# Block 0 of a hybrid encoder layer: x taken channel-major and unnormalised, and the memory's product moved behind the convolution

## The chip, the cores and the metric

The kernel runs on one core of one Trainium2 chip. The metric is the device time of one execution in microseconds (us); where several executions are given, their median is what counts. Matmuls run on TensorE (PE in the profile), elementwise work on VectorE (DVE), ScalarE (ACT) and GpSimd (POOL); SyncE (SP) issues most transfers. All numbers are float32.

## The reference

One encoder layer on 2048 tokens of 1024 channels. Three mixers read the same normalised input, are gated and added, and an MLP follows. Cut to what the change touches:

```python
h = rmsnorm(x, g_mix)                    # x / rms(x), times a gain for each channel
z = h @ w_in
qk_m, v_m, o_m, i_pre, f_pre, qkv_na, q_mem, gate_pre = jnp.split(z, split_idx, axis=-1)
qk_m = jax.nn.silu(short_conv(qk_m, conv_w, conv_b))       # 5 taps along the tokens
q_na = rmsnorm(q_na[:, :, 0], g_na_q) * (NA_HEAD_DIM ** -0.5)
k_na = rmsnorm(k_na[:, :, 0], g_na_k)
h_mem = memory_cross_attention(q_mem, rmsnorm(mem, g_mem), w_mem_kv, g_mem_q, g_mem_k)
    # k, v = split(mem_n @ w_mem_kv); softmax(q k^T) v over 256 memory tokens, 4 heads of 64
gates = jax.nn.sigmoid(gate_pre).reshape(bsz, s, N_BRANCH, D_MODEL)
y = gates[:, :, 0] * (h_m @ w_proj_mlstm) + gates[:, :, 1] * (h_na @ w_proj_na) \
    + gates[:, :, 2] * (h_mem @ w_proj_mem)
x = x + y @ w_out
return x + jnp.square(jax.nn.relu(rmsnorm(x, g_ffn) @ w_up)) @ w_down
```

1/rms is one number per token, so it commutes with the product by w_in: (x * g) @ w, scaled by 1/rms of the token afterwards, is the same result.

## The kernel before

**Products in three.** Every large product takes both operands as a high and a low part (`hi`, `lo`, written as fp32r: `hi` is the rounded copy, `lo` what is left) and issues three matmuls, hi*hi, hi*lo and lo*hi (lines 242, 243, 244, `mm3`). A weight comes as units of 512 KB: `fetch` loads one into a raw buffer (`wr`, three of them), ACT writes hi (line 185), DVE writes lo (line 186) into a split buffer (`ws`, five of them). `take(4)` hands four units to a group of products, and loads run ahead in the order of a list (`wplan`). A split buffer comes free when the last product that reads it is done.

**Stages.** The 2048 tokens are four blocks of 512. The first phase goes through the blocks; in each block (`block_a`) PE computes, with the block's normalised, transposed x (`hT`, hi and lo): naqk (queries and keys of the neighbourhood attention; four tiles of 128 tokens, 24 products each), four units of the convolution (channel-major, 24 products each, line 697 moves the result to `cz`, then five taps on DVE, lines 705 to 710, and a tanh on ACT, line 709), navm (values of the neighbourhood attention and the memory's queries; two groups for each tile, `ev` from line 537 and `zm`, `zif` from lines 545 and 546), v, the mLSTM's gates for some blocks, and o. A second phase runs the mLSTM with the branch gates (line 625) of two more blocks, blocks 1 and 0, as filling; a third does projections and the MLP. PE's order is written by hand: between the products of a group, `tick` draws work from a list of jobs and from two streams of attention units (one of neighbourhood attention's q and k, one with two lanes of memory units). The other engines' orders come from a scheduler that goes by the order of the program and its dependences.

**x in block 0 and in the others.** Blocks 1 to 3 get x twice: token-major for the sums of squares (line 462), channel-major (`xT`) for the product. 1/rms is spread over all partitions by a product with ones (line 476), x is scaled on DVE (line 431) and split. Block 0 gets x token-major: squares on ACT (line 350), scaling on DVE (line 352), 32 transposes on PE (line 358, in groups of four), and 32 + 32 small moves to hi and lo (lines 363 and 364).

**The start.** The first product is the memory's: `mem_setup` loads memT, splits it into the buffer of `hT` (lines 1174, 1175) and multiplies it with w_mem_kv (48 products into two PSUM banks, named mx) while x of block 0 comes in. Then come naqk's tiles in the order 2, 3, 0, 1. Of the PSUM banks in this phase `mm` has 2, `tr` 3 and `mx` 3. A memory unit (`mem_unit`) takes two mx banks for its scores (12 small products, line 1275), DVE takes the maxima (line 1278), ACT the exponentials (line 1282).

## Time and profile before

| | |
|---|---|
| median of three runs | 2867.02 us (2867.16, 2867.02, 2863.83) |
| profiled execution, its own time | 2865.11 us |
| span of that execution | 2863.4 us |
| PE busy | 2844.4 us, 99% |
| DVE busy | 2046.7 us, 71% |
| ACT busy | 1163.9 us, 41% |
| granted clock, mean | 0.999 |

Times in the profile are microseconds from the start of the span. A row of the timeline gives the start, the duration, the engine, the line of the kernel, what is written and read, and in brackets how long the engine stood idle before it and what released it. A PE row's duration is longer than the time to the next row, since products overlap: what a product costs is the distance of starts, 0.23 us for 512 columns and 0.12 us for 256. A row of the waits gives the total, the number and the longest of the waits of that kind.

### The profile page before, as it was taken

To read this page: it belongs to the slowest core of one execution; us is meant where nothing else is said; L and a number is where in the kernel's file an instruction comes from. 1 tells how busy PE (TensorE), PEld (TensorE's weight loads), DVE (VectorE), ACT (ScalarE), POOL (GpSimd) and SP (SyncE) were. 2 spreads that over 40 slices of the span, in tenths; PEclk is the share of its full clock that TensorE was granted. 3 is DMA by queue.
4 is the path that set the end of the run, shared out by engine and by line. 5 is a ranking of instruction groups with operands and counts; after the bars stand their busy time and mean duration, and the time that the engine had idled before them with its cause. 6 is when DMAs were issued, how large, how long until landed. Compare 5 with 4: busy or idle time off the path is not lost.

```text
span 2863.4 us, 41480 instructions
## 1 busy us (share of the span) xinstructions
PE 2844.4 (99%) x14950; PEld 2355.7 (82%) x14950; DVE 2046.7 (71%) x3522; ACT 1163.9 (41%) x2205; POOL 199.0 (7%) x254
## 2 busy tenths in 40 slices
PE   9999999999999999999999999999999999999999
PEld 7888888888887888888888888888888888888887
DVE  7686865477765555647699888866786998887666
ACT  6464654355544433532343334333223433343331
POOL 3221210011000122310000000000000000000000
PEclk9999999999999999999999999999999999999999
DMA  8686777886899888977444447756773444476553
GB/s 294 210 281 208 248 238 245 263 245 204 281 312 310 266 271 265 308 262 267 121 152 149 149 162 244 242 196 229 256 219 121 152 149 149 162 249 230 196 188 133
DMA packets 345149, 631.70 MB, mean 221 GB/s; under 512 B 29584, under 2 KB 151376, under 8 KB 344944
## 3 DMA queue, kind: packets, MB, share of 16 engines
q1 hardware_dynamic: 344528, 628.79, 66.9%
q8 instruction: 118, 1.93, 0.3%
q14 instruction: 87, 0.71, 0.1%
q10 hardware_dynamic: 416, 0.27, 0.0%
HBM read 452.32 MB, written 176.62 MB: 220 GB/s over the span
## 4 chain that ended last, share of the span: by engine, by line
PE 92%; DVE 3%; DMA 2%; issue 1%; ACT 1%; POOL 0%; SPq 0%; ACTq 0%; DVEq 0%; POOLq 0%
PE mm L242 28%; PE mm L244 27%; PE mm L243 27%; PE tr L1130 2%; DMA wr<-in_w_units_dram 1%; PE pn L902 1%; PE mx L1144 1%; PE mx L1110 1%; PE pn L905 1%; PE mx L911 1%; PE mx L1305 1%; PE tr L1295 1%; PE mx L1275 1%; DVE ws L186 0%; DVE cy L707 0%
## 5 line engine op out<-in xcount | busy, mean ns | idle before, releaser
L242 PE MATMUL mm<-X,ws 128*128 128x512 f32 x896 | 349.5, 390 | 0.2 <-ACT u L1499 0.2
L243 PE MATMUL mm<-X,ws 128*128 128x512 f32 x896 | 348.6, 389 | 0.0
L244 PE MATMUL mm<-X,ws 128*128 128x512 f32 x896 | 348.6, 389 | 0.0
L186 DVE TENSOR_TENSOR ws<-wr,ws 128x1024 fp32r<-128x1024 f32 (+2 forms) x195 | 237.5, 1225 | 124.3 <-ACT ws L185 122.7
L242 PE MATMUL mm<-hT,ws 128*128 128x512 f32 (+1 forms) x776 | 304.8, 393 | 1.4 <-DMA hT<-s_hT 1.4
L244 PE MATMUL mm<-hT,ws 128*128 128x512 f32 (+1 forms) x776 | 301.7, 389 | 0.0
L243 PE MATMUL mm<-hT,ws 128*128 128x512 f32 (+1 forms) x776 | 301.4, 388 | 0.0
L185 ACT ACTIVATE ws<-wr 128x1024 fp32r<-128x1024 f32 (+2 forms) x195 | 204.6, 1055 | 192.6 <-PE mm L244 135.7
L244 PE MATMUL mm<-X 128*128 128x512 f32 x616 | 239.7, 389 | 0.5 <-DVE X L1563 0.5
L242 PE MATMUL mm<-X 128*128 128x512 f32 x616 | 239.7, 389 | 0.0
L243 PE MATMUL mm<-X 128*128 128x512 f32 x616 | 239.6, 389 | 0.0
L242 PE MATMUL mm<-ws,hT 128*128 128x512 f32 (+2 forms) x640 | 226.4, 354 | 2.7 <-ACT ws L185 1.6
L212 ACT ACTIVATE ws<-wr 128x512 fp32r<-128x512 f32 x224 | 133.9, 627 | 232.8 <-PE mm L244 145.6
L243 PE MATMUL mm<-ws,hT 128*128 128x512 f32 (+2 forms) x640 | 223.3, 349 | 2.1 <-DVE ws L186 2.1
L244 PE MATMUL mm<-ws,hT 128*128 128x512 f32 (+2 forms) x640 | 223.6, 349 | 0.1
L1562 ACT ACTIVATE X<-X 128x1024 fp32r<-128x1024 f32 x109 | 115.7, 1062 | 209.4 <-DMA X<-s_s 92.5
L242 PEld LDWEIGHTS mm<-X,ws 128*128 128x128 f32 x896 | 168.2, 188 | 36.0 <-ACT u L1499 0.6
L243 PEld LDWEIGHTS mm<-X,ws 128*128 128x128 f32 x896 | 168.2, 188 | 35.3 <-issue 0.5
L244 PEld LDWEIGHTS mm<-X,ws 128*128 128x128 f32 x896 | 168.2, 188 | 34.8
L1579 DVE TENSOR_TENSOR acc<-acc,mm 128x512 f32<-128x512 f32 x192 | 126.3, 682 | 70.0 <-PE mm L244 70.0
L1563 DVE TENSOR_TENSOR X<-X 128x1024 fp32r<-128x1024 f32 x109 | 132.4, 1222 | 58.0 <-ACT X L1562 57.4
L242 PEld LDWEIGHTS mm<-hT,ws 128*128 128x128 f32 x776 | 146.1, 188 | 31.0 <-issue 2.8
(280 smaller groups left out, 5946.1 us busy)
## 6 DMA issues: line engine op xcount, KB each, us to landing
wr<-in_w_units_dram SPq DMA_DIRECT2D x289, 512.0 KB
s_s<-u SPq DMA_DIRECT2D x32, 1024.0 KB
s_g<-ev SPq DMA_DIRECT2D x96, 256.0 KB
ev<-s_g SPq DMA_DIRECT2D x96, 256.0 KB
s_a<-u SPq DMA_DIRECT2D x96, 256.0 KB
X<-s_s SPq DMA_DIRECT2D x45, 512.0 KB
nab<-in_rpb_dram SPq DMA_DIRECT2D x96, 220.0 KB
xt<-in_w_units_dram SPq DMA_DIRECT2D x32, 512.0 KB
```

The costliest lines, as they stand in the source:

```text
L185: s = nc.scalar.activation(w[:, 0, ks], raw[:, ks], AF.Copy)
L186: v = nc.vector.tensor_tensor(w[:, 1, ks], raw[:, ks], w[:, 0, ks].bitcast(F32), ALU.subtract)
L212: nc.scalar.activation(hi, src, AF.Copy)
L242: mm(out, lhs[0], rhs[0], start=first, stop=False)
L243: mm(out, lhs[0], rhs[1], start=False, stop=False)
L244: mm(out, lhs[1], rhs[0], start=False, stop=last)
L902: mm(pn[h % 2][:, h // 2], pt[:, h], v1[:, h], start=h < 2, stop=first)
L905: mm(pn[h % 2][:, h // 2], qw[hp, h // 2], C[hp, h // 2], start=False, stop=True)
L1130: nc.tensor.transpose(ptp[0:120, j], sb[:, j * 120:(j + 1) * 120], self.ident)
L1562: nc.scalar.activation(hi, src, AF.Copy)
L1563: nc.vector.tensor_tensor(lo, src, hi.bitcast(F32), ALU.subtract)
L1579: nc.vector.tensor_tensor(c, first[t] if first else c, p, ALU.add)
```

## The change

The change has these parts.

- The memory's product is no longer first. `first_loads` loads x of block 0 channel-major (`xT`, 2 MB), times the gain but without 1/rms, and splits it into `hT` (lines 1141 and 1142 of the changed kernel, 8 + 8 moves for each half of the block). `first_tiles` multiplies naqk's tiles 0 and 1 with it in two mx banks, step by step as the weights arrive, then tiles 2 and 3.
- The four transposed tiles of block 0 are gone: no scaling of rows, no transposes on PE, no 32 + 32 small moves. x is still loaded token-major (2 MB) for the sums of squares.
- `first_rms` computes 1/rms, keeps it per token (`r0`, with 0.5/rms in its second half) and spreads it over the partitions with one product with ones (`rb0`), which is also stored and loaded again in the second phase.
- 1/rms goes into block 0's results: as the scale of the moves of navm, v and o, as a factor on the sums of squares and on the scale in the neighbourhood attention's q and k (one more small POOL operation), as a product on DVE with `rb0` in the convolution's move (line 663, before on ACT), and in the 24 gates of block 0 in the second phase as a product on DVE (line 585), with the tanh on ACT behind it, in place.
- The memory's input is loaded by jobs during the convolution (`mem_load`), its 48 products (`mem_kv`) come between the convolution and navm, and its weights stand behind the convolution's in the list. So the memory units of block 0 start later.

```diff
-        out = list(u["w_mem_kv"])
+        out = []
         for b in range(NB):
-            for n in ("naqk", "qk", "navm", "v"):
+            for n in ("naqk", "qk") + ("w_mem_kv",) * (b == 0) + ("navm", "v"):
                 out += u[n]
...
+            rb=d("s_rb", [128, TB]),
...
-    def prep(self, xt, out, junk):
-    def trans_part(self, xh, dst, t, g):
-    def trans(self, xh, dst, t, later=0):
-    def load_norm(self, src, xt=None):
...
-        self.xorder = [(0, t) for t in ORDER_0] + [(b, t) for b in range(1, NB) for t in range(4)]
+        self.xorder = [(b, t) for b in range(1, NB) for t in range(4)]
         self.xhs = []
         self.hT = self.p_h.tile([128, 2, 8, TB], F32R, name="hT", tag="hT", bufs=1)
         self.streams = [self.unit_stream(self.qkq, [(1, 3)]), self.unit_stream(self.memq, [(3,), (3,)]), self.na_stream()]
-        self.mem_setup()
+        w = self.first_loads()
...
+        self.first_tiles(w)
...
-        w = self.take(4)
-        for i, t in enumerate(ORDER_0 if b == 0 else range(4)):
-            if i == 0 or b == 0 and i < 3:
+        rt = lambda t: self.r0[:, t:t + 1] if b == 0 else 1.0
+        w = self.take(4) if b else ()
+        for t in range(4) if b else ():
+            if t == 0:
                 self.trans_x()
-            if b == 0 and i == MEM_R:
-                self.mem_rms()
             p = self.tok_group(hT, w, t)
             z = self.t("zna", [128, 512], 4)
             self.out = nc.scalar.activation(z, p, AF.Copy).ins,
             self.qkq.append(self.na_qk(b, t, z.rearrange("p (a b) -> p a b", b=32)))
+        if b == 0:
+            mem = self.mem_load()
+            self.jobs += [lambda: next(mem, None)] * 16
...
+        if b == 0:
+            self.mem_kv()
...
-            self.out = nc.scalar.activation(s, p, AF.Copy).ins,
+            self.out = nc.scalar.activation(s, p, AF.Copy, scale=rt(t)).ins,
...
-            v = nc.vector.tensor_copy(z, p[:, 0:256])
-            self.out = v.ins, nc.scalar.activation(zif[:, t], p[:, 256:272], AF.Copy).ins
+            v = nc.vector.tensor_scalar(z, p[:, 0:256], rt(t), None, ALU.mult) if b == 0 else nc.vector.tensor_copy(z, p[:, 0:256])
+            self.out = v.ins, nc.scalar.activation(zif[:, t], p[:, 256:272], AF.Copy, scale=rt(t)).ins
...
-            self.out = nc.scalar.activation(s, p, AF.Copy).ins,
+            self.out = nc.scalar.activation(s, p, AF.Copy, scale=rt(t)).ins,
...
-            self.out = nc.scalar.activation(s, p, AF.Tanh, scale=0.5).ins,
+            self.out = nc.scalar.activation(s, p, AF.Tanh, scale=0.5 if b else self.r0[:, 4 + t:5 + t]).ins,
...
-        self.out = self.nc.scalar.activation(s, p, AF.Tanh, scale=0.5).ins,
+        if b == 0:
+            self.out = self.nc.vector.tensor_tensor(s, p, self.rb, ALU.mult).ins,
+            self.nc.scalar.activation(s, s, AF.Tanh, scale=0.5)
+        else:
+            self.out = self.nc.scalar.activation(s, p, AF.Tanh, scale=0.5).ins,
...
+        self.rb = self.gbc[:, 0:TB]
+        nc.sync.dma_start(self.rb, self.scr["rb"])
...
-        self.out = nc.scalar.activation(z[:, 4:4 + TB], p, AF.Copy).ins,
+        if b == 0:
+            self.out = nc.vector.tensor_tensor(z[:, 4:4 + TB], p, self.rb0, ALU.mult).ins,
+        else:
+            self.out = nc.scalar.activation(z[:, 4:4 + TB], p, AF.Copy).ins,
...
-        nc.scalar.activation(sq, z, AF.Square)
+        r0 = self.r0[:, t:t + 1] if b == 0 else 1.0
+        nc.scalar.activation(sq, z, AF.Square, scale=r0)
         ss = self.small(16, "q")
         nc.vector.tensor_reduce(ss, sq, AX.X, ALU.add)
         r = self.rstd(ss, 32, "q")
+        if b == 0:
+            nc.gpsimd.tensor_scalar(r, r, r0, None, ALU.mult)
...
-    def mem_setup(self):
+    def first_loads(self):
...
+        xs = [p_a.tile([128, 4 * 704], F32, name=f"xs{i}", tag="nak", bufs=2)[:, :2 * D].rearrange("p (t c) -> p t c", t=2) for i in range(2)]
+        src = [a["xT"][2 * i:2 * i + 2].rearrange("t p c -> p t c") for i in range(2)]
+        def split(i, k):
+            hi, lo = (self.hT[:, l, k, i * 256:i * 256 + 256].rearrange("p (t c) -> p t c", t=2) for l in range(2))
+            x, g = xs[i][:, :, k * 128:(k + 1) * 128], self.gmix[:, k:k + 1]
+            nc.scalar.activation(hi, x, AF.Copy, scale=g)
+            nc.vector.scalar_tensor_tensor(lo, x, g, hi.bitcast(F32), ALU.mult, ALU.subtract)
         later, self.later = self.later, 0
         for k in range(0, 8, 2):
             if k == 0:
                 self.fetch(2)
...
+            cs = slice(k * 128, k * 128 + 256)
+            (nc.sync if k else nc.scalar).dma_start(xs[0][:, :, cs], src[0][:, :, cs])
             for i in (k, k + 1):
...
+                split(0, i)
             if k:
                 self.fetch()
...
+        for k in range(0, 8, 4):
+            cs = slice(k * 128, k * 128 + 512)
+            nc.sync.dma_start(xs[1][:, :, cs], src[1][:, :, cs])
+        self.later = later
+        self.xr = []
+        for t in range(4):
+            self.n += 1
+            x = self.x_tile(a["x"][t * 128:t * 128 + 128]) if t < 2 else p_a.tile([128, D], F32, name=f"xr{t}", tag="naq", bufs=2)
+            if t > 1:
+                nc.sync.dma_start(x, a["x"][t * 128:t * 128 + 128])
+            self.xr.append(x)
+        for k in range(8):
+            split(1, k)
         w = self.take(4)
...
+        self.r0 = p_a.tile([128, 8], F32, name="r0")
+        return w
+    def first_rms(self):
+        nc = self.nc
+        ss = self.small(4, "x")
+        for t, x in enumerate(self.xr):
+            nc.scalar.activation(x, x, AF.Square, accum_out=ss[:, t:t + 1])
+            yield
+        r = self.rstd(ss, D, "x")
+        nc.gpsimd.tensor_copy(self.r0[:, 0:4], r)
+        nc.gpsimd.tensor_scalar(self.r0[:, 4:8], r, 0.5, None, ALU.mult)
+        yield
+        self.rb0 = self.gbc[:, 0:TB]
+        dg = self.ev().rearrange("p (t c) -> p t c", t=4)
+        nc.vector.tensor_tensor(dg, self.ident.unsqueeze(1).to_broadcast([128, 4, 128]),
+                                r.unsqueeze(2).to_broadcast([128, 4, 128]), ALU.mult)
+        for _ in range(7):
+            yield
+        p = self.ps("tr")
+        nc.tensor.matmul(p, self.ones, dg.rearrange("p t c -> p (t c)"), start=True, stop=True)
+        nc.scalar.activation(self.rb0, p, AF.Copy)
+        self.store(self.scr["rb"], self.rb0)
+    def first_tiles(self, w):
+        nc, hT = self.nc, self.hT
+        rms = self.first_rms()
+        self.jobs += [None] * RMS_0 + [lambda: next(rms, None)] * 13
+        zs = [self.t("zna", [128, 512], 4) for _ in range(4)]
+        unit = lambda t: self.qkq.append(self.na_qk(0, t, zs[t].rearrange("p (a b) -> p a b", b=32)))
         ps = [self.ps("mx") for _ in range(2)]
...
         for k in range(8):
             wk = w[k // 2]
             for t in range(2):
...
+                self.mm3(ps[t], self.lhs_tok(hT, k, t), (wk[:, 0, k % 2], wk[:, 1, k % 2]), k == 0, k == 7)
             self.tick()
...
+        self.out = tuple(nc.scalar.activation(z, p, AF.Copy).ins for z, p in zip(zs, ps))
+        for t in (2, 3):
+            p = self.tok_group(hT, w, t)
+            self.out = nc.scalar.activation(zs[t], p, AF.Copy).ins,
+            unit(t - 2)
+        unit(2)
+        unit(3)
+    def mem_load(self):
+        nc, a, p_a = self.nc, self.a, self.p_a
+        raw = [p_a.tile([128, D], F32, name=f"memT{i}", tag="naq", bufs=2) for i in range(2)]
+        for i in range(2):
+            nc.sync.dma_start(raw[i].rearrange("p (k t) -> p k t", k=4), a["memT"][i * 512:(i + 1) * 512].rearrange("(k p) t -> p k t", p=128))
+        yield
+        mt = [self.x_tile(a["mem"][t * 128:t * 128 + 128]) for t in range(2)]
+        self.memT = [p_a.tile([128, 4 * 704], F32R, name=f"memh{i}", tag="nak", bufs=2)[:, :2 * D].rearrange("p (k t) -> p k t", k=8)
+                     for i in range(2)]
+        for _ in range(MEM_LOAD):
+            yield
+        for k in range(8):
+            x, g = raw[k // 4][:, k % 4 * 256:k % 4 * 256 + 256], self.gmem[:, k:k + 1]
+            hi, lo = (m[:, k] for m in self.memT)
+            nc.scalar.activation(hi, x, AF.Copy, scale=g)
+            nc.vector.scalar_tensor_tensor(lo, x, g, hi.bitcast(F32), ALU.mult, ALU.subtract)
+            yield
+        ss = self.small(2, "x")
+        for t in range(2):
+            nc.scalar.activation(mt[t], mt[t], AF.Square, accum_out=ss[:, t:t + 1])
+        self.rm = self.rstd(ss, D, "m")
+    def mem_kv(self):
+        nc = self.nc
+        w = self.take(4)
+        ps = [self.ps("mx") for _ in range(2)]
+        for k in range(8):
+            wk = w[k // 2]
+            for t in range(2):
+                ts = slice(t * 128, (t + 1) * 128)
+                self.mm3(ps[t], tuple(m[:, k, ts] for m in self.memT), (wk[:, 0, k % 2], wk[:, 1, k % 2]), k == 0, k == 7)
+            self.tick()
+        out = []
         for t, p in enumerate(ps):
             z = self.t("zm", [128, 256], 4)
...
+            out.append(nc.scalar.activation(z, p[:, 0:256], AF.Copy).ins)
+            out.append(nc.vector.tensor_copy(self.mv[:, t], p[:, 256:512]).ins)
+            self.memq.append(self.mem_keys(t, z, self.rm[:, t:t + 1]))
+        self.out = tuple(out)
```

Three places show how the order moves. The first is **PE in naqk of block 0**, between the first tiles in the rows of before (`mm_574` is a tile's PSUM bank, `ws_296` and `ws_301` are weight buffers, `tr_600` a bank of transposed x).

```order
L244 MATMUL mm_574<-ws_296,hT 128x512
L358 MATMUL tr_600<-ident,xstage 128x128 x4
L242 MATMUL mm_574<-ws_301,hT 128x512
L243 MATMUL mm_574<-ws_301,hT 128x512
L244 MATMUL mm_574<-ws_301,hT 128x512
```

In the changed kernel, from the last products of tile 2 to the first of tile 3:

```order
L242 MATMUL mm_421<-ws_268,hT 128x512
L243 MATMUL mm_421<-ws_268,hT 128x512
L241 MATMUL mm_447<-ws_230,hT 128x512
L242 MATMUL mm_447<-ws_230,hT 128x512
L243 MATMUL mm_447<-ws_230,hT 128x512
```

The groups of four transposes are gone, and the weights of tiles 0 and 1 (`ws_230` to `ws_268`) serve tiles 2 and 3 too. The second place is **ACT at the end of block 0's navm**. Before, with `mm_1142` the second group of tile 2, `zif` its move by ACT, `ws_936` to `ws_946` the high parts of v's weights and `mq_1253` the queries of a memory unit:

```order
L1244 ACTIVATE sq_1169<-zm_1106 128x4x64
L546 ACTIVATE zif_955<-mm_1142 128x16
L537 ACTIVATE ev_1221<-mm_1179 128x256
L986 ACTIVATE stq_1020<-tr_1205,gna 128x2x64
L185 ACTIVATE ws_936<-wr_935 128x2x512
L185 ACTIVATE ws_941<-wr_940 128x2x512
L185 ACTIVATE ws_946<-wr_945 128x2x512
L986 ACTIVATE stq_1020<-tr_1205,gna 128x2x64
L1257 ACTIVATE mq_1253<-tr_1254,gmqk 128x256
```

In the changed kernel, with `mm_1053` the second group of tile 2, `ev_1126` the move of tile 3's first group and `mk` the memory's keys:

```order
L496 ACTIVATE ev_1126<-mm_1084,r_332 128x256
L1278 ACTIVATE sq_1163<-zm_952 128x4x64
L1278 ACTIVATE sq_1175<-zm_1018 128x4x64
L184 ACTIVATE ws_832<-wr_831 128x2x512
L184 ACTIVATE ws_837<-wr_836 128x2x512
L184 ACTIVATE ws_842<-wr_841 128x2x512
L1291 ACTIVATE mk<-tr_1158,gmqk 128x2x128
L1291 ACTIVATE mk<-tr_1170,gmqk 128x2x128
L505 ACTIVATE zif_851<-mm_1053,r_332 128x16
```

Tile 2's `zif` stood ahead of the three weights and now stands behind them and behind the keys. The third place is **DVE at the first memory units of block 0**. Before, with `mx_1328` and `mx_1329` the two score banks of the first unit and `mq_1360` the queries of the second:

```order
L1278 TENSOR_REDUCE sm_1342<-mx_1328 128x2
L1278 TENSOR_REDUCE sm_1343<-mx_1329 128x2
L1258 SCALAR_TENSOR_TENSOR mq_1360<-tr_1361,gmqk,mq_1360 128x256
L1286 RECIPROCAL sm_1354<-sm_1344 128x2
L1287 TENSOR_TENSOR me_1348<-me_1348,sm_1354 128x512
```

In the changed kernel, with `mx_1336`, `mx_1337` the banks of the first unit and `mx_1368`, `mx_1369` those of the second:

```order
L1292 SCALAR_TENSOR_TENSOR mq_1284<-tr_1285,gmqk,mq_1284 128x256
L1292 SCALAR_TENSOR_TENSOR mq_1290<-tr_1291,gmqk,mq_1290 128x256
L1312 TENSOR_REDUCE sm_1350<-mx_1336 128x2
L1312 TENSOR_REDUCE sm_1351<-mx_1337 128x2
L1320 RECIPROCAL sm_1362<-sm_1352 128x2
L1321 TENSOR_TENSOR me_1356<-me_1356,sm_1362 128x512
L1320 RECIPROCAL sm_1365<-sm_1353 128x2
L1321 TENSOR_TENSOR me_1359<-me_1359,sm_1365 128x512
L1312 TENSOR_REDUCE sm_1382<-mx_1368 128x2
L1312 TENSOR_REDUCE sm_1383<-mx_1369 128x2
```

The two lanes of memory units, which stood a step apart, now go in step: both queries are there before the first scores, and on PE the 24 score products of two units stand one behind the other, twice in block 0.

More of the change, by code (lines that the diff above doesn't have):

```diff
@@ L431, in prep_x @@
                 nc.vector.scalar_tensor_tensor(xt[:, k], xt[:, k], self.gmix[:, k:k + 1], rb, ALU.mult, ALU.mult)
-            self.xhs.append((xt, t, True))
+            self.xhs.append((xt, t))
     def trans_x(self, later=1):
         if self.xhs:
-            xh, t, major = self.xhs.pop(0)
-            if not major:
-                self.trans(xh, self.hT, t, later)
-                return
+            xh, t = self.xhs.pop(0)
             self.jobs += [None] * (later - len(self.jobs) - 1)
@@ L1196, in mem_setup @@
         nc.vector.tensor_copy(self.gmqk[:, 1:2], gq[:, 1:2])
+        self.gmem = p_a.tile([128, 8], F32, name="gmem")
+        nc.sync.dma_start(self.gmem, a["g_mem"])
         self.mk = p_a.tile([128, 2, 2, 256], F32R, name="mk")
         self.mv = p_a.tile([128, 2, 256], F32, name="mv")
-        ps = [self.ps("mx") for _ in range(2)]
-        self.trans_x(MEM_T)
-        turns = self.jobs[-2:]
-        def turn(f, marks):
-            with self.queued(marks()):
-                f()
-        self.jobs[-2:] = [lambda f=f: turn(f, lambda: first) for f in turns]
-        self.jobs += [lambda i=i: turn(lambda: self.prep_x(xt=xs[:, i * D:(i + 1) * D]), lambda: self.turned + second) for i in range(2)]
+        self.r0 = p_a.tile([128, 8], F32, name="r0")
[26 more added lines that the diff above has]
+        unit = lambda t: self.qkq.append(self.na_qk(0, t, zs[t].rearrange("p (a b) -> p a b", b=32)))
+        ps = [self.ps("mx") for _ in range(2)]
         for k in range(8):
```

72 lines of the change are left out of this document (3 added, 69 removed).

## The prediction

> **What bounds the kernel now.** I read the page's busy times first, then PE's waits, then the windows of the first block, the only stretch in which the order on PE changes much.
>
> ```profile
> span 2863.4 us, 41480 instructions
> PE 2844.4 (99%) x14950; PEld 2355.7 (82%) x14950; DVE 2046.7 (71%) x3522; ACT 1163.9 (41%) x2205; POOL 199.0 (7%) x254
> ```
>
> PE is busy for all but 19 us of the span. An edit gains only what it takes out of PE's products or out of these 19 us. The waits of PE that the change touches (engine, line, releaser: total, times, longest):
>
> ```profile
> PE mm L243 <- DVE ws L186: 2.1, 3, 0.8
> ...
> PE mm L242 <- ACT ws L185: 1.6, 1, 1.6
> PE mx L243 <- DVE ws L186: 1.5, 2, 0.8
> ...
> PE mm L242 <- ACT zif L546: 1.0, 2, 0.8
> ```
>
> The first three say that PE waits for split weights, the fourth that it waits in navm for a PSUM bank to be emptied. Windows of 20 us (window, length, busy PE, PEld, DVE, ACT, POOL, clock, DMA share, GB/s) show where:
>
> ```profile
> 0.00:20.00 20.00, 16.89 (x72) 13.69 (x73) 13.39 (x31) 13.27 (x22) 2.17 (x9) 1.00 0.91 332
> 20.00:40.00 20.00, 17.03 (x76) 13.21 (x75) 13.12 (x33) 15.94 (x36) 7.15 (x9) 0.91 0.77 271
> ...
> 60.00:80.00 20.00, 20.00 (x115) 17.52 (x114) 19.25 (x33) 8.71 (x16) 8.29 (x5) 1.00 0.96 314
> ```
>
> In 0 to 40 us PE is short of weights while the DMA engines are nearly full. From 60 on PE is full, and so nearly is DVE, which does the taps of the convolution there: DVE is the engine that falls behind next.
>
> **Removed: the starvation at the start.** PE's timeline:
>
> ```profile
> 13.10 0.39 PE L242 MATMUL mx<-ws,hT 128*128 128x512 f32 x1
> 14.28 0.50 PE L243 MATMUL mx<-ws,hT 128*128 128x512 f32 x1 [0.79 <-DVE ws L186]
> ...
> 21.70 0.39 PE L244 MATMUL mm<-ws,hT 128*128 128x512 f32 x1
> 23.68 0.49 PE L242 MATMUL mm<-ws,hT 128*128 128x512 f32 x1 [1.59 <-ACT ws L185]
> 24.94 0.80 PE L243 MATMUL mm<-ws,hT 128*128 128x512 f32 x1 [0.77 <-DVE ws L186]
> 25.53 0.63 PE L244 MATMUL mm<-ws,hT 128*128 128x512 f32 x1
> ...
> 27.24 0.87 PE L358 MATMUL tr<-ident,xt 128*128 128x128 f32 x4
> ...
> 29.68 0.48 PE L242 MATMUL mm<-ws,hT 128*128 128x512 f32 x1
> 30.77 0.50 PE L243 MATMUL mm<-ws,hT 128*128 128x512 f32 x1 [0.61 <-DVE ws L186]
> ```
>
> A product costs 0.23. From 13.10 to 14.28 one ran: 0.95 lost. From 21.70 to 27.24 seven ran: 5.54 - 1.61 = 3.93 lost, 1.2 of it since products were 0.43 apart after the two stalls. At 29.68, a product that takes 0.31 behind transposes, 0.78. Together 5.7. Here two groups of weights, eight units, are used up in 26 us. In the changed kernel four units feed all four tiles of naqk, 96 products or 22 us, and the fifth is wanted at about 6 + 22 + 2 = 30. Until then 2 MB of xT, 2 MB of x and five units, 2.5 MB, must come: 6.5 MB at the 332 GB/s of the first window are 20 us. So I take the whole 5.7. The other end: if the loads of x delay the units as much as memT did, half stays, 2.8.
>
> **Removed: 32 transposes, eight groups like this one.**
>
> ```profile
> 16.91 0.60 PE L358 MATMUL tr<-ident,xt 128*128 128x128 f32 x4
> 17.27 0.48 PE L242 MATMUL mx<-ws,hT 128*128 128x512 f32 x1
> 17.58 0.40 PE L243 MATMUL mx<-ws,hT 128*128 128x512 f32 x1
> ```
>
> 0.36 for the group and 0.08 for the slower product behind it make 0.44, times 8: 3.5. Nothing covers PE, so this is certain. The moves and scalings that go with them ran on ACT and DVE beside PE and count nothing by themselves.
>
> **Removed and put back: navm's waits.**
>
> ```profile
> 83.79 0.28 PE L244 MATMUL mm<-ws,hT 128*128 128x256 f32 x1
> 84.25 0.39 PE L242 MATMUL mm<-ws,hT 128*128 128x272 f32 x1 [0.17 <-ACT zif L546]
> ...
> 90.17 0.28 PE L244 MATMUL mm<-ws,hT 128*128 128x256 f32 x1
> 91.29 0.39 PE L242 MATMUL mm<-ws,hT 128*128 128x272 f32 x1 [0.84 <-ACT zif L546]
> ```
>
> Starts of 0.12 would be free, so these cost 0.34 and 1.00, 1.3 in all. With other orders on ACT and DVE the second group of tile 1 now takes the bank that the first group just filled, and its move stands on ACT behind the last unit's tanh, which waits for the taps on DVE. How late are they? Groups of DVE, the first from the page, the others from its first 110 us:
>
> ```profile
> L1579 DVE TENSOR_TENSOR acc<-acc,mm 128x512 f32<-128x512 f32 x192 | 126.3, 682 | 70.0 <-PE mm L244 70.0
> ...
> L186 DVE TENSOR_TENSOR ws<-wr,ws 128x1024 fp32r<-128x1024 f32 x16 | 19.2, 1222 | 4.5 <-ACT ws L185 4.4
> L707 DVE SCALAR_TENSOR_TENSOR cy<-cz,cws,cy 128x512 f32<-128x512 f32 x16 | 12.3, 770 | 0.3
> ...
> L1175 DVE SCALAR_TENSOR_TENSOR hT<-memT,gmem,hT 128x256 fp32r<-128x256 f32 x8 | 3.4, 477 | 0.0
> ```
>
> Between the convolution's first move and navm the change gives DVE the low parts of four memory weights (4.9), the memory's eight splits (3.8), four moves of `cz` like L1579's (2.7) and scalings of some 1.5: 12.9. PE gets 48 products, 11.0, beside which they can run. So DVE comes 1.9 later, counted from PE, on top of the first wait's 0.34: 2.2 for navm's waits. Low end 0.3 (as the first before), high end 1.0 + 1.9 = 2.9 and 0.4 for a second group behind it, 3.3. I take 2.1.
>
> **Added: one product with ones,** as block 1 has:
>
> ```profile
> 79.78 1.02 PE L476 MATMUL tr<-zna,ones 128*128 128x512 f32 x2
> 80.63 0.60 PE L977 MATMUL tr<-ident,zna 128*128 128x128 f32 x4
> ```
>
> 0.85, both ends alike. The POOL operation in the attention's norms, the scales on ACT's moves and the load of `rb` wait on no engine that PE needs soon. The 24 moves of gates on DVE in the second phase, 24 x 0.68 = 16 us, are hidden: DVE is busy for 60 of 100 there.
>
> ```profile
> 1100.00:1200.00 100.00, 60.50 (x140) 1.00 0.93 296
> ```
>
> Without that cover each could cost PE up to the 0.68.
>
> **Added: the first v group waits.** It takes the bank of tile 2's second group, whose `zif` now stands behind three weights, and these can only start when the last navm group lets go of their buffers. Before, the three took (ACT, then DVE):
>
> ```profile
> 98.61 2.96 ACT L185 ACTIVATE ws<-wr 128x1024 fp32r<-128x1024 f32 x3 [0.38 <-PE mm L244]
> ...
> 99.70 3.50 DVE L186 TENSOR_TENSOR ws<-wr,ws 128x1024 fp32r<-128x1024 f32 x3 [0.96 <-ACT ws L185]
> ```
>
> The group of 24 products (3.0) frees the first buffer after 0.75. DVE ends 1.09 + 3.50 = 4.6 later, at 5.3, `zm` and `zif` take 0.4 + 0.2: 5.9. PE has the group and two pairs of transposes until 3.9. That is 2.0, and 0.2 for DVE being late: 2.2. Low end 0.8 (DVE not needed behind the third weight), high end 3.0.
>
> **Added: two pairs of memory units.** 24 scores run through, which want four banks of mx where there are three. Before, one unit's scores and what empties them:
>
> ```profile
> 106.43 0.97 PE L1275 MATMUL mx<-mk,mq 64*128 64x256 f32 x12
> ...
> 107.44 1.29 DVE L1278 TENSOR_REDUCE sm<-mx 128x2 f32<-128x512 f32 x2 [0.56 <-PE mx L1275]
> ...
> 108.18 0.47 ACT L1282 ACTIVATE me<-mx,sm 128x256 f32<-128x256 f32 x1
> ...
> 108.63 0.47 ACT L1282 ACTIVATE me<-mx,sm 128x256 f32<-128x256 f32 x1
> ```
>
> The scores end at 107.34 (106.43 and 0.91 to the next start) and the first bank is empty at 109.1: 1.7 us that the second unit's scores wait. Twice: 3.4. Low end 1.0 (if one pair comes apart in time), high end 5.0 (ACT or DVE busy with weights when the maxima are due).
>
> **The sum:** -5.7 - 3.5 - 1.3 + 0.85 + 2.1 + 2.2 + 3.4 = -2.0. The low ends give -5.7 - 3.5 - 1.3 + 0.85 + 0.3 + 0.8 + 1.0 = -7.6, the high ends -2.8 - 3.5 - 1.3 + 0.85 + 3.3 + 3.0 + 5.0 = +4.6. Against the profiled execution's 2865.11: 2863.1, ends 2857.6 and 2869.7. The median shown is 1.9 above that execution, the fastest run 1.3 below it; I keep to 2863.1.
>
> **The rivals.**
>
> *The new waits are hidden* (0.24). Then -5.7 - 3.5 - 1.3 + 0.85 = -9.6 and some 1 of rest: 2856.5. For it: the trace shows no wait of PE for scores or for `zif` in later blocks. Against: no later block has two units in step, or `zif` behind the weights.
>
> *DVE becomes the bound of block 0* (0.10). From the first `cz` to navm's third move PE has three units, the 48 products and three navm groups: 16.5 + 11.0 + 9 = 37 us. DVE has the taps (12.3), nine weights (11.0), the memory's splits (3.8), `cz` (2.7) and, an estimate from the count of smaller operations, some 12: 42. It is 19.25 of 20 busy in 60 to 80 already. If it also starts late, since the first `cz` needs 1/rms of all four tiles, all moves behind it come late by as much: navm's wait becomes 9, v's 3.0, the scores' 5.0, and -5.7 - 3.5 - 1.3 + 0.85 + 17 = +7.4, or 2872.5; it is slower by over 0.2% once DVE is 9 us behind PE in navm, and at 11 it is 2874.5.
>
> *The clock drops behind each new wait* (0.09). After 1.59 and 0.77 of idleness, five products from 23.68 lost 1.2. If each of the four new waits did this, +4.8: 2867.9. Against it, a longer single wait in the second phase:
>
> ```profile
> 860.90 0.38 PE L1110 MATMUL mx<-nak,naq 96*128 96x320 f32 x1 [1.70 <-DMA nak<-s_ks]
> 861.12 0.39 PE L242 MATMUL mm<-hT,ws 128*128 128x512 f32 x1
> ```
>
> The next product is 0.22 later, at full clock. The Trainium skill (TensorE: Matmul & The Clock Gate, Part 1: The HAM clock gate) has the clock halve after an idle window of about 3.4 us; by that no wait of 2.2 costs more than itself, and these rows agree. It would only bear on DVE's case.
>
> *The start stays starved* (0.05): 2.8 to 5.7 are not gained, 2866 to 2869.
>
> **How the numbers follow.** The sum's case has 0.52, in its own range 2859.5 to 2867. A measurement of this kernel tells about 0.2% from no change, 5.7 us: faster is below 2861.3, slower above 2872.7. Below 2861.3 lie the hidden waits (0.22 of 0.24) and the lower part of the sum's case (0.09): 0.31. Above 2872.7 lie DVE's case (0.07) and a trace of the others (0.02): 0.09. The rest is 0.60. The range for 8 in 10 takes in the hidden waits and the high ends of the sum: 2855.5 to 2869.5.
>
> **What would show it.** Right: PE's timeline from 13 to 36 us without a stall; no transposes of x; a wait of 1 to 3 at navm's second groups, with the move of line 496 as releaser; one of 2 at v's first product behind `zif` (line 505); two of 1.7 at line 1309. Wrong: no wait at 1309 or v (hidden); a wait at line 663's `cz`, or of over 4 in navm (DVE); products 0.43 apart behind the waits (clock); a wait for `ws` before 30 us (start).

## The result, and the profile after

| | before | after |
|---|---|---|
| median (executions) | 2865.98 us (4, 2863.83 to 2867.16) | 2905.58 us (4, 2902.88 to 2906.77) |
| span of the profiled execution | 2863.4 us | 2904.4 us |
| PE busy | 2844.4 us | 2874.5 us |

The ratio is 1.0138, with a 95% interval of 1.0126 to 1.0151: 40 us slower, where 2 us were forecast to be gained. The head of the page after:

```profile
span 2904.4 us, 41435 instructions
PE 2874.5 (99%) x14920; PEld 2357.8 (81%) x14920; DVE 2063.0 (71%) x3531; ACT 1164.7 (40%) x2186; POOL 202.9 (7%) x254
```

PE has 30 instructions fewer and is busy 30.1 us longer. So most of the 41.0 us are not waits: products have become slower. To see where, the same product is looked up in both traces. PE's place is its start after less its start before, at times on the clock of before:

| | 86 us | 205 | 406 | 608 | 1004 | 2001 | 2806 |
|---|---|---|---|---|---|---|---|
| after | -9.2 | +3.5 | +6.1 | +10.9 | +12.9 | +28.0 | +41.2 |

Read as differences: the start gains (-9.8 at 80 us). The stretch from there to 205 us loses 13.3; it holds the rest of block 0 and the first products of block 1, among which block 0's last memory units run. What is left of the first phase loses 9.2 (the place is +12.7 at 965 us), the second phase 2.3, the third 26.2.

**The third phase.** Windows of PE in the third phase (length, busy time and number of instructions, clock, DMA share, GB/s), after:

```profile
1300.00:1400.00 100.00, 100.00 (x430) 1.00 0.68 230
1500.00:1600.00 100.00, 100.00 (x427) 1.00 0.46 156
1800.00:1900.00 100.00, 100.00 (x443) 1.00 0.72 248
```

and before:

```profile
1300.00:1400.00 100.00, 100.00 (x443) 1.00 0.60 194
1500.00:1600.00 100.00, 100.00 (x443) 1.00 0.44 150
1800.00:1900.00 100.00, 100.00 (x442) 1.00 0.62 211
```

PE never stands still in any of them, the clock is full, and yet after has 427 products where before has 443. From 1800 to 1900 both have the same. The timeline after says which products these are. First nine products whose two operands lie in different buffers, then nine with both in X:

```profile
1509.56 0.40 PE L243 MATMUL mm<-X,ws 128*128 128x512 f32 x1
...
1511.66 0.40 PE L243 MATMUL mm<-X,ws 128*128 128x512 f32 x1
...
1850.06 0.39 PE L241 MATMUL mm<-X 128*128 128x512 f32 x1
...
1852.10 0.39 PE L241 MATMUL mm<-X 128*128 128x512 f32 x1
```

With X and the weight `ws` the nine take 2.10, so starts are 0.233 apart; with both operands in X they take 2.04, 0.227 each. The timeline before has nine products of X with `ws` in 2.04 us too:

```profile
1509.70 0.39 PE L244 MATMUL mm<-X,ws 128*128 128x512 f32 x1
...
1511.74 0.39 PE L244 MATMUL mm<-X,ws 128*128 128x512 f32 x1
```
The source lines of this phase are the same in both kernels; only the place of the tiles in SBUF differs, as the experiments show.

**Block 0.** PE's timeline after, at the places that the prediction names (the rows at 167 and 184 us are block 0's memory units, but stand among the first products of block 1):

```profile
67.11 0.38 PE L242 MATMUL mm<-ws,hT 128*128 128x256 f32 x1 [0.60 <-DVE ws L185]
...
75.01 0.39 PE L241 MATMUL mm<-ws,hT 128*128 128x272 f32 x1 [0.77 <-ACT ev L496]
...
88.45 0.39 PE L241 MATMUL mm<-ws,hT 128*128 128x272 f32 x1 [0.18 <-ACT ev L496]
...
95.28 0.80 PE L241 MATMUL mm<-ws,hT 128*128 128x512 f32 x1 [3.12 <-ACT zif L505]
95.87 0.63 PE L242 MATMUL mm<-ws,hT 128*128 128x512 f32 x1
96.30 0.63 PE L243 MATMUL mm<-ws,hT 128*128 128x512 f32 x1
...
116.63 0.97 PE L1309 MATMUL mx<-mk,mq 64*128 64x256 f32 x11 [1.72 <-ACT me L1316]
...
167.20 0.97 PE L1309 MATMUL mx<-mk,mq 64*128 64x256 f32 x11 [1.72 <-ACT me L1316]
...
184.34 0.90 PE L1101 MATMUL tr<-ident,nsb 128*120 128x128 f32 x3 [2.83 <-ACT mpT L1331]
...
185.30 0.63 PE L241 MATMUL mm<-hT,ws 128*128 128x512 f32 x1
```

Between 2 and 67 us there are no other waits than two of 0.30 and 0.76, at 5.79 and 10.29: the start is as forecast, and better. Behind the waits of 3.12 and 2.83 products start 0.43 apart for some 3 us, which costs another 1.6 and 1.3; behind the two of 1.72 they don't here. Together: 0.95 in navm's banks, 0.60 for a weight, 4.7 at v, 3.4 at the scores, 4.1 at `mpT`.

**The other blocks.** The single largest loss is at one weight in block 2, PE's timeline after:

```profile
588.99 0.49 PE L241 MATMUL mm<-ws,hT 128*128 128x512 f32 x1 [2.73 <-ACT ws L184]
590.25 0.79 PE L242 MATMUL mm<-ws,hT 128*128 128x512 f32 x1 [0.76 <-DVE ws L185]
```

Before, the first of these two products does not wait, and the second waits the same 0.76 (at 581.02). The next largest after are waits of 1.27 at 310 us and 1.51 at 393 us, where before has none, and one of 1.79 at 873 us with slow products behind it, where before waits 1.70 without them.

### The profile page after: what moved, and what is told of

The parts are those of the page before. It is cut to its first block, busy times and chain, and to the rows that moved or that the text cites. A ratio compares the mean times of both kernels' runs of the same rounds, so it can differ in the third digit from the quotient of the medians.

```text
span 2904.4 us, 41435 instructions
## 1 busy us (share of the span) xinstructions
PE 2874.5 (99%) x14920; PEld 2357.8 (81%) x14920; DVE 2063.0 (71%) x3531; ACT 1164.7 (40%) x2186; POOL 202.9 (7%) x254
## 2 busy tenths in 40 slices
DMA packets 347054, 634.33 MB, mean 218 GB/s; under 512 B 29696, under 2 KB 152512, under 8 KB 346848
## 4 chain that ended last, share of the span: by engine, by line
PE 93%; DVE 3%; DMA 2%; issue 1%; ACT 1%; SPq 0%; POOL 0%; DVEq 0%; ACTq 0%; POOLq 0%
PE mm L241 28%; PE mm L243 28%; PE mm L242 28%; PE tr L1101 2%; PE mx L1115 1%; PE pn L870 1%; PE mx L1081 1%; DMA wr<-in_w_units_dram 1%; DVE ws L185 1%; PE pn L873 1%; PE mx L879 1%; PE mx L1339 1%; PE tr L1329 0%; PE mx L1309 0%; DMA xt<-in_x_dram 0%
## 5 line engine op out<-in xcount | busy, mean ns | idle before, releaser
L241 PE MATMUL mm<-X,ws 128*128 128x512 f32 x896 | 355.2, 396 | 0.0
L242 PE MATMUL mm<-X,ws 128*128 128x512 f32 x896 | 354.4, 395 | 0.0
L243 PE MATMUL mm<-X,ws 128*128 128x512 f32 x896 | 354.3, 395 | 0.0
L241 PE MATMUL mm<-ws,hT 128*128 128x512 f32 (+2 forms) x624 | 220.8, 354 | 6.8 <-ACT zif L505 3.1
L242 PE MATMUL mm<-ws,hT 128*128 128x512 f32 (+2 forms) x624 | 217.5, 349 | 1.4 <-DVE ws L185 1.4
L243 PE MATMUL mm<-ws,hT 128*128 128x512 f32 (+2 forms) x624 | 217.7, 349 | 0.0
L241 PEld LDWEIGHTS mm<-X,ws 128*128 128x128 f32 x896 | 168.3, 188 | 41.2 <-issue 0.5
```

The costliest lines, as they stand in the source:

```text
L241: mm(out, lhs[0], rhs[0], start=first, stop=False)
L242: mm(out, lhs[0], rhs[1], start=False, stop=False)
L243: mm(out, lhs[1], rhs[0], start=False, stop=last)
```

## The experiments

PE's place against before in each, as in the table above; the kernels are described below.

| | 86 us | 205 | 406 | 608 | 1004 | 2001 | 2806 |
|---|---|---|---|---|---|---|---|
| after | -9.2 | +3.5 | +6.1 | +10.9 | +12.9 | +28.0 | +41.2 |
| e1: after, aligned | -8.5 | +3.6 | +5.0 | +10.2 | +9.0 | +9.0 | +9.7 |
| e2: before, 32 bytes off | -0.3 | -0.2 | +1.5 | +2.2 | +2.3 | +17.3 | +31.1 |
| e4: e1, keys staggered | -8.4 | -4.2 | +4.0 | +11.5 | +13.4 | +13.3 | +15.3 |
| e5: e1, other buffers | -9.1 | -3.0 | +2.3 | +10.4 | +9.8 | +9.8 | +10.5 |
| e6: both | -8.2 | -5.7 | -1.8 | +4.6 | +7.0 | +6.9 | +9.7 |
| e7: e6, time given back | -8.7 | +1.8 | +5.1 | +9.9 | +9.4 | +9.4 | +10.1 |
| e12: before, weights sooner | +0.1 | -0.5 | -0.1 | -1.5 | +11.4 | +14.6 | +18.9 |
| e13: before, 28 products more | -0.4 | +9.3 | +9.4 | +9.7 | +9.6 | +9.1 | +10.0 |
| e15: e6, two loads sooner | -8.6 | -4.5 | +0.3 | +6.4 | +6.8 | +6.7 | +7.5 |

**Addresses.** `PAD` (line 30) is the size of a tile that nobody reads, laid ahead of B in the pool of the second and third phase. The change frees 288 bytes of small buffers in the pool ahead of it, so that B, hB and X, which lie behind, moved down by 288 (X from 129792 to 129504), while `ws` and `hT` stayed: what was a whole number of 128-byte steps between X and `ws` is now 32 off. e1 is the changed kernel with these tiles back on such a step:

```diff
-PAD = 256
+PAD = 288
```

> The changed kernel with 32 bytes more of padding ahead of B and X: their start moves from 96736 and 129504 bytes of a partition (32 past a multiple of 64) to 96768 and 129536 (multiples of 64). Nothing else moves. Theory (address): products whose moving operand starts 32 bytes off a multiple of 64 are 0.2333 us apart instead of 0.2267, and that is all that the third phase lost; the distance of products there is 0.2267 again, and 26 us of the third phase and some 1.5 us of the second phase's products with hB come back: 2878 us, between 2875 and 2881, still 10 to 14 above the kernel before. Rival (company): the products of the third phase are slower for what runs beside them, since the changed block 0 shifts transfers and splits against PE; then the distance stays 0.2333 and the time 2903 to 2907.

Median 2878.11 us (2874.63 to 2879.99), ratio to before 1.0040 (1.0025 to 1.0055). Its windows:

```profile
1300.00:1400.00 100.00, 100.00 (x443) 1.00 0.64 216
```

27.5 us of the median come back, and by PE's place 27.6 us behind 1004 us. e2 is the counter-test, the same edit made to the kernel before:

> The kernel before, with 32 bytes more of padding ahead of B and X (to 97056 and 129824 bytes, 32 past a multiple of 64); every instruction and its order is the same. Theory (address): the third phase's products with X and B go from 0.2267 to 0.2333 us, and the time rises by 26 to 28 us, to 2893 (2890 to 2896). Rival (company): no change, 2864 to 2868.

2894.50 us (2892.86 to 2895.64), ratio 1.0097 (1.0080 to 1.0114), and its windows look like those of after:

```profile
1300.00:1400.00 100.00, 100.00 (x432) 1.00 0.61 202
1500.00:1600.00 100.00, 100.00 (x427) 1.00 0.42 145
```

32 bytes alone cost 28 us in a kernel in which nothing else is edited. e3 asks whether steps of 64 would do (`PAD = 320` in before):

> The kernel before with 64 bytes more of padding (B and X at 97088 and 129856 bytes: multiples of 64, not of 128). If a multiple of 64 is what the moving operand needs, the distance of products stays 0.2267 and the time 2864 to 2868; if it needs 128, 0.2333 and 2893. The rival (company) expects no change here either, so this run only tells how wide the line is.

2884.88 us (one execution). They don't: 20 of the 28 us are lost. e8 moves all pools of before by 32 together, `ws` and `hT` too (`self.pad(self.p_ws, 160)` for 128), so that no distance changes:

> The kernel before with 32 bytes more of padding ahead of all pools: weights, hT, X and B all start 32 bytes past a multiple of 64, and their distances from each other stay as they were. If what counts is where the moving operand starts, every product of 512 columns is 0.2333 apart and the time 2866 + 11600 x 0.0066 = 2943 us or so. If what counts is the distance of the moving operand's start from the stationary one's (a multiple of 128 or not), nothing changes: 2864 to 2868.

2866.88 us (one execution), as before. So it is the distance between the two operands that counts, not where either lies. The distance of starts of products of 512 columns of X, B or hB with `ws`, by how far the moving operand's address lies from the stationary one's, modulo 128 bytes: 226.7 ns at 0 (before, e1, e8), 233.3 at 32 (e2) and at 96 (after), and at 64 (e3) two paces, 228.9 and 233.3, with a mean of 231.4. Products with both operands in X keep 226.7 in all of them.

**Block 0's waits.** Two edits in e1, each for one cause. e4 staggers the memory's two lanes, in `mem_keys` behind the transposes, so that two units don't ask for banks together:

```diff
         self.mem_trans(z, self.mk[:, :, :, t * 128:(t + 1) * 128], self.gmqk[:, 1:2])
+        for _ in range(t):
+            yield
+            yield
```

> The changed kernel with the padding and with the second memory key unit yielding four times more, but the memory's z still in zm's buffers. It measures the price of the paired memory units alone. At the product that the kernel before starts at 202 us, padding alone stands 3.6 us behind the kernel before, padding with both edits 6.1 ahead. Expected here: no wait at line 1309 and none for mpT, 3.4 + 2.1 + 1.3 less, so 3.3 us ahead at that product; the first v group's wait of 3.1 stays. If the two edits only help together, it is behind by more than 1.

2879.99 us (one execution). The waits at line 1309 and at `mpT` are gone, the one at `zif` stays (3.10), and PE stands nearly 8 better at 205 us. e5 takes the other cause: the memory's keys use two of `me`'s buffers, so that navm finds `zm`'s four free.

```diff
-            z = self.t("zm", [128, 256], 4)
+            z = self.t("me", [128, 2, 256], 4)[:, 0]
```

> The changed kernel with the padding and with the memory's z in buffers of the tag me, the lanes in step as in the change. It measures the first v group's wait alone. If that wait comes from zm's four buffers (navm's third zm waits until the transposes of the memory's keys, right ahead of the v group on PE, have freed one), it is gone, 3.1 and 1.6 of slow products: 1.1 us ahead of the kernel before at the product of 202 us, with the two waits of 1.7 at line 1309 still there. If it comes from the three weights ahead of zif on ACT and DVE, as the prediction had it, a wait of 2 or more stays.

2875.49 us (one execution). The wait at `zif` is gone entirely, though the three weights are split at the same time. Rows of DVE say why. In the changed kernel `zm`'s move stands behind the weights:

```profile
90.61 3.91 DVE L185 TENSOR_TENSOR ws<-wr,ws 128x1024 fp32r<-128x1024 f32 x3 [0.54 <-ACT ws L184]
94.44 0.47 DVE L504 TENSOR_SCALAR zm<-mm,r 128x256 f32<-128x256 f32 x1
```

In e5 the same move of the same tile stands ahead of them:

```profile
84.35 0.48 DVE L504 TENSOR_SCALAR zm<-mm,r 128x256 f32<-128x256 f32 x1 [5.37 <-PE mm L243]
...
90.76 3.91 DVE L185 TENSOR_TENSOR ws<-wr,ws 128x1024 fp32r<-128x1024 f32 x3 [0.53 <-ACT ws L184]
```

With two of `zm`'s buffers held by the keys until their transposes on PE (91.56), that move can't be sooner. It is the prediction's wait, then, but for want of a buffer. The wait for `mpT` shrinks here as well, from 2.10 in e1 to 0.54 (at 179.32), though the two units still make their eight transposes together. In after, ACT's move for `mpT` stands behind work that had to wait 1.69 for a load of x (at 178.98), and so does e1's (0.96 at 178.89); in e5 it doesn't. So the pairing alone does not make that wait. The two of 1.72 at line 1309 stay, and behind one of them the products now start 0.43 apart:

```profile
111.76 0.97 PE L1309 MATMUL mx<-mk,mq 64*128 64x256 f32 x11 [1.72 <-ACT me L1316]
...
113.02 0.63 PE L241 MATMUL mm<-ws,hT 128*128 128x512 f32 x1
113.44 0.63 PE L242 MATMUL mm<-ws,hT 128*128 128x512 f32 x1
```

e6 has both edits:

> The changed kernel with the padding of the run before, and two edits in block 0: the second memory key unit yields four times more, so that the two lanes of memory units stand apart by two of their steps, and the memory's z is put into two buffers of the tag me instead of zm, so that navm's third zm needs not wait until the memory's z have been transposed. Theory (block 0's waits are its own): the wait of the first v group (3.1 and 1.6 of slow products behind it), the two waits for scores (1.7 each) and the wait of transposes for mpT (2.8 and some 1.3) go, 12 us: 2866 against 2878 for padding alone, between 2861 and 2869; below 2864 if the waits of the later blocks (1.3, 1.2 and 4.3 more than before) are also gone. Rival (DVE is the bound of block 0): the waits come back at other places, and the time is 2874 to 2880.

2876.61 us (2874.76 to 2881.40), ratio 1.0039 (1.0024 to 1.0054). The waits named above are gone, and PE stands at -5.7 at 205 us, 9.3 better than e1. Of the expected 12 us the rest is lost to a new wait, of 1.85 at 126 us for the bank that v's move (line 516) empties, with slow products behind it; e7, e15 and e16 have it too. The total did not follow: what was gained is lost again by 608 us (+4.6) and 1004 us (+7.0). The largest wait:

```profile
582.76 0.49 PE L241 MATMUL mm<-ws,hT 128*128 128x512 f32 x1 [3.87 <-ACT ws L184]
584.03 0.80 PE L242 MATMUL mm<-ws,hT 128*128 128x512 f32 x1 [0.77 <-DVE ws L185]
```

**The later blocks.** PE's order in blocks 1 to 3 is the same in all kernels, but the scheduler gave other orders to the other engines (matched by tile names, some 390 of SP's 1852 issues stand elsewhere in e6's trace than in before's). Does PE, arriving sooner, run into loads that come at their own pace? e7 gives the time back: e6 with 28 products of ones, which nobody reads, at the end of block 0.

```diff
             self.block_a(b)
+            if b == 0:
+                p = self.ps("mx")
+                for _ in range(28):
+                    nc.tensor.matmul(p[:, 0:128], self.ones, self.ones, start=True, stop=True)
```

> The kernel with padding, stagger and buffers, with 28 products of ones with ones (128 columns, results read by nobody) on PE at the end of block 0, some 6.4 us by the warming products' 0.23 at full clock. It gives back what block 0 won over the kernel before, so that PE comes to the later blocks when the kernel before does. If the later blocks lose time because PE comes too early for transfers that have their own pace, they lose nothing here: 2866 to 2869, and the wait at 582 us is under 1. If they lose it because the queues and engines work in another order since the change, the loss of some 13 us comes again: 2879 to 2884.

2875.72 us (one execution): neither. Between 205 and 1004 us it loses 7.6 where e6 loses 12.7, so some of that loss may depend on the arrival; the end is the same.

Three runs change the scheduler's numbers in e6: how late the sums of the MLP's weights stand (`LOW` from 100 to 300, e9), how late the weights do (`LATER` from 60 to 20, e10), and both (e11). e12 is before with `LATER = 20`.

> The changed kernel with padding, stagger and buffers, and the preparation of the third phase's weight sums in the first phase put lower in the scheduler's order (its number LOW from 100 to 300). PE's order stays. In every kernel with the change so far PE waited 2.4 to 5.0 us at about 585 us for one weight (0.8 before), whose transfer stood close behind two others on SP. By the order, the two others are now loaded 8 and 12 us of PE's time earlier. Theory (the later blocks lose by the order that the scheduler gives SP, ACT and DVE): the wait at 585 falls under 1 us, the slow products behind it go, 5 us: 2871, between 2868 and 2873. Rival (they lose by the 2.6 MB more that the change loads, or by PE's earlier arrival): the wait comes back there or elsewhere, 2875 to 2878.

> The same kernel (padding, stagger, buffers), with LOW as it was, and the weights' loads and splits put higher in the scheduler's order (LATER from 60 to 20). That weight is then loaded 16.6 us of PE's time ahead of its first use instead of 11.1, and split 5.0 ahead instead of 1.8. Theory (order): as for the run before, the wait at 585 under 1 us, 2868 to 2873. Rival (bytes or arrival): 2875 to 2878.

> Both edits of the order together, on the kernel with padding, stagger and buffers. That weight is loaded 29.9 and split 11.1 us ahead. Theory (order): no wait at 585, and 2862 to 2870, as fast as the kernel before if the smaller waits of the later blocks go too. Rival: 2875 to 2878.

> The control: the kernel before with LATER from 60 to 20 and nothing else. It tells whether the edit of the order helps any kernel or only mends what the change brought about. The kernel before waits 0.8 us at that weight, so it can gain 1 us there: 2863 to 2867. If the edit itself is worth 5 us, it comes to 2861 or below.

2887.99 (ratio 1.0081), 2891.07 (1.0091), 2897.89 (1.0105) and 2881.08 us (1.0057). In e9 and e10 the wait at 585 is gone, as the order says, and larger ones stand elsewhere, in e10 for example

```profile
608.57 0.79 PE L241 MATMUL mm<-ws,hT 128*128 128x512 f32 x1 [6.00 <-ACT ev L541]
643.13 0.70 PE L1081 MATMUL mx<-nak,naq 96*128 96x440 f32 x1 [6.21 <-DMA nab<-in_rpb_dram]
```

The same number hurts the kernel before too (+15.6 us). It is no remedy, and these runs don't tell the order from the change.

e13 and e14 do. They are the kernel before with the products of e7's diff (28, and 112): bytes, addresses and PE's order stay, PE arrives later, and some 50 rows of SP, 30 of ACT and 60 of DVE stand elsewhere.

> The kernel before, with 28 products of ones by ones of 128 columns (read by nobody, some 0.06 us each, 1.7 us together) at the end of block 0. Nothing else is edited: same bytes, same stages, same SBUF addresses. PE's order is that of before but for the 28; the scheduler writes some 50 rows of SP, 30 of ACT and 60 of DVE in another order. Theory (the later blocks' loss comes from the order that the scheduler gives SP, ACT and DVE, and any edit ahead of them changes it): at 1000 us this kernel stands clearly behind before by more than its own products, +4 to +10, and the wait at 585 us is longer than before's 0.76; time 2870 to 2876. Rival (the loss is the change's own: its 2.6 MB more, or the place in which its jobs stand): +1.7 at 1000 us and at the end, 2867.6, and waits at 585, 866 and 929 us as before.

> As the kernel with 28, but 112 such products, some 6.9 us. Theory (order): +10 to +17 at 1000 us, 2875 to 2883, with the same kind of longer waits near 585 us. Rival (the change's own): at most +6.9, and less if the loads that PE waits for at 585, 866 and 929 us arrive in the time that the products give them: 2869 to 2873.

2875.68 us (2874.56 to 2881.80), ratio 1.0039 (1.0026 to 1.0051), and 2896.82 us (one execution). The products' price was mis-sized: 0.22 us each, 6.3 for the 28, behind a wait of 2.85 for their bank. But the question is answered: +9.3 at 205 us and +9.6 at 1004, +31.7 and +32.9. Neither a later arrival nor the other order of some hundred rows costs the later blocks more than 1.2 us. My theory that any edit ahead of them costs them several us falls. What is left is the change's own: particular rows of the queues, which it moves far more of, or the bytes that it adds. Its page counts 634.33 MB where before's has 631.70, and between PE's places of 205 and 608 us it moves some 1.4 MB more (99.9 against 98.5). No run here takes the bytes away and leaves the order.

Which rows could it be, for the wait at 583? In SP's queue of e6 the two weights ahead of the awaited one are issued at 559.61 and 565.84, just ahead of its own issue at 572.55; before, they are out by 554.85 and the awaited one follows at 572.02. DMA's share, before:

```profile
560.00:570.00 10.00, 10.00 (x50) 8.33 (x49) 4.77 (x14) 3.38 (x6) 0.00 (x0) 1.00 0.79 253
570.00:580.00 10.00, 9.91 (x46) 7.90 (x44) 4.14 (x12) 3.70 (x8) 0.00 (x0) 1.00 0.97 291
```

and in e6:

```profile
560.00:570.00 10.00, 10.00 (x50) 8.31 (x49) 6.03 (x11) 4.11 (x8) 0.00 (x0) 1.00 0.98 338
570.00:580.00 10.00, 8.90 (x41) 6.99 (x40) 6.47 (x17) 3.09 (x6) 0.00 (x0) 1.00 1.05 253
```

Before, the awaited weight is split at 578.66, 6.6 us behind its issue, and ACT does not wait for the load there, so that it took 6.6 at most. In e6 it is split at 581.66, 9.1 behind its issue, and there ACT waits for the load. e15 moves those two loads, with their splits, forward in e6, and no other row; e16 the awaited one as well, behind which some 40 rows of SP move.

```diff
-        self.tc.cur_priority = prio + self.later
+        self.tc.cur_priority = prio + (later := 0 if 1028 <= self.n <= 1040 else self.later)
...
-        self.tc.cur_priority -= self.later
+        self.tc.cur_priority -= later
```

(In e16 the number is -60, and the range reaches to 1048.)

> The kernel with the addresses aligned, the staggered key transposes and the other buffers (2876.6), in which only two loads of SP's queue stand further ahead: the two weights before the one that PE waits for at 583 us (3.87 us). Each moves ahead of a few rows of the queue, its split likewise on ACT and DVE; no other row of any engine moves. Theory (the wait at 583 is a matter of the queue's order: in the changed kernels these two weights are issued late, at 560 and 566 us, so their transfers share the DMA engines with the awaited one): that one lands sooner, the wait falls to 0.8 to 2.0 and the slow products behind it go; 2 to 4.7 us less, 2872 to 2875. Rival (the awaited weight is late whatever goes before it, since its own issue at 572 us stays): wait 3.5 to 4.2, time 2875 to 2878.

> As the kernel with two loads sooner, but the awaited weight's load as well: it can be issued 22.7 us of PE's time ahead of its use (11.1 before). Some 40 rows of SP, 20 of ACT and 30 lines of DVE move behind it. Theory: no wait at 583, 4 to 6 us less there, 2871 to 2873, if the weight behind it (which can be issued 11.1 us ahead now, 23.4 before) doesn't take the wait over. Rival (the wait moves on to that next weight at 609 us, as with the numbers changed for all weights): 2875 to 2882.

e15: 2872.61 us (2870.75 to 2877.47), ratio 1.0028 (1.0018 to 1.0039).

```profile
584.50 0.50 PE L241 MATMUL mm<-ws,hT 128*128 128x512 f32 x1 [2.40 <-ACT ws L184]
585.76 0.50 PE L242 MATMUL mm<-ws,hT 128*128 128x512 f32 x1 [0.76 <-DVE ws L185]
```

The wait falls from 3.87 to 2.40, between what the theory and the rival expected: the two loads account for some 1.5 us of it, in this one trace; the ratios of e6 and e15 overlap. The awaited one, issued at 575.13 here and split at 583.40, still takes 8.3. e16: 2883.30 us (2881.11 to 2885.77), ratio 1.0058 (1.0042 to 1.0075); its wait at 583 is gone, and 5.89 and 6.57 stand at 611 and 646. The first is the rival's in place and, at one remove, in cause: PE waits for a bank whose move on ACT (line 541) stands behind a split, and the split waits 2.91 for its weight. The second, for a load of `nak`, neither had, and the time is 1.3 above the rival's range.

No version beats before. The best of the changed ones, e15, is 0.28% slower.

## Why the prediction was wrong

It forecast 2863.1, in 2855.5 to 2869.5, with 0.09 for slower; 2905.6 was measured. By its steps:

- **The start and the transposes: right, too small.** -5.7 - 3.5 + 0.85 = -8.4 were forecast, PE's place at 80 us is -9.8, with a wait of 0.60 for a weight (67.11) in it that was not foreseen.
- **Navm's waits: right place, half the size.** The waits for the bank that line 496 empties are 0.77 and 0.18 long, 0.95 together, for 2.1. The first has the forecast cause: the move of line 496 starts at 74.50 on ACT, behind the last tanh (73.71), which waited for DVE's taps. So DVE was late by less than 1.9. The rival of DVE as the bound of block 0 is out: from 60 to 80 us DVE is still busy for 18.62 of 20, but then it stands idle for 9.92 (up to 88.74), and is at 8.80 of 20 from 80 to 100.
- **The first v group: right place and releaser, 4.7 for 2.2.** The wait is 3.12 (upper end 3.0) and the slow products behind it cost 1.6. The trace shows the move behind three weights, as forecast; e5 shows that it stands there for want of a `zm` buffer, which the prediction did not see.
- **The scores: right to 0.02.** Two waits of 1.72 at line 1309, for 1.7 each, one unit waiting for the other's exponentials. e4 takes them away with the stagger.
- **Left out: the units' second half.** The pairs meet once more, at the banks for their transposed exponentials: 2.83 and 1.3 at 184 us, in part because ACT comes late there (e5). The step "two pairs of memory units" counted the scores only.
- **The clock rival (0.09): right in part, and wrongly argued against.** "No wait of 2.2 costs more than itself" rested on a rule and on one wait of 1.70. Of the new waits of over 1 us up to 205 us, the two longest (3.12 and 2.83) dropped the clock in this execution, the two of 1.72 did not, and in e5 one of 1.72 did. By the rule that the prediction cited from the Trainium skill (TensorE: Matmul & The Clock Gate, Part 1: The HAM clock gate), an idle window of about 3.4 us, none of these would; the traces differ.
- **The step that failed: the sum itself.** It added up block 0's terms, -2.0, and took everything behind as equal, since the products there are the same lines. Block 0 comes to +3.5, 5.5 off. The other 37.7 us of PE's place lie behind it. 27.5 are the addresses (after against e1), and e2 puts such a price on 32 bytes alone. Some 9 in this trace (5 in e1's) are the later blocks, where PE's order is the same but the order of the queues and the bytes moved are not. No rival named either.

How the loss in the later blocks divides is settled in part. A later arrival of PE and a light reshuffle cost nothing (e13, e14). Two loads that stand later in SP's queue go with 1.5 us of the wait at 583 (e15, one trace), and where the weights were moved ahead, larger waits came up elsewhere, some of them for other loads (e10, e12, e16). What the rest is stays open, and so does whether the added bytes have a part in it: e15 still loses 11.3 between 205 and 1004 us in several waits of 1 to 2.4 us. Up to 500 us, ahead of its edit, it runs the same order as e6 and lies up to 3.2 us from it there, so a single trace doesn't tell waits of that size apart; the clock behind a wait is one reason why.

## What to carry to other kernels

A change in one stage can move the tiles of all others: when small buffers go or come, look at where the operands of the large products land, and hold their distance at a multiple of 128 bytes by a pad; here that was worth more than all that the change did on purpose. If PE has more busy time with fewer instructions, look for slower products before looking for waits. And in a kernel that is 99% busy, do not take the stages behind an edit as equal because PE's order there is: here they lost some 5 to 9 us with the same products. The order in the DMA queue is one place to look, though it is shown only for a part of one wait.

## What the runs showed of the hardware

- Products of 128x512 in fp32r start 226.7 ns apart when the addresses of the moving and the stationary operand differ by a multiple of 128 bytes, 233.3 ns when they are 32 or 96 off, and 228.9 or 233.3 at 64. e8, with both moved together, keeps the 226.7. The cause inside the chip no run shows.
- A wait of PE of 2 us or less can be followed by products of 512 columns that start 0.43 apart, and whether it is differs between executions of the same stretch. In the 18 traces the granted clock then stands at 0.5 for 3.41 us, at some waits for two or three times that; behind after's waits of 3.12 and 2.83 it cost 1.6 and 1.3 us. Counted behind 20 us, it fell at 10 of 34 waits of 1.5 to 2.0 us (four of them before's pair of 1.59 and 0.77, in seven traces that have it), at 15 of 19 of 2.0 to 2.7, and at 25 of 26 longer ones. The granted clock of a window shows it too, after:

```profile
80.00:100.00 20.00, 16.70 (x106) 14.83 (x105) 8.80 (x15) 8.33 (x16) 8.12 (x9) 0.91 0.69 221
100.00:120.00 20.00, 18.28 (x99) 14.86 (x98) 5.47 (x12) 5.68 (x18) 0.00 (x0) 1.00 0.74 248
```

The first window holds the wait of 3.12, the second the first of 1.72. A wait should be costed with this surcharge by its chance.
